# A cheaper score step in the attention's budget, a copy moved to ScalarE, and one more step between x row loads and their use

## The chip, the cores and the metric

The kernel runs on 1 core of one Trainium2 chip. The core has five engines with instruction queues of their own: TensorE (PE, with its weight loads shown apart as PEld), VectorE (DVE), ScalarE (ACT), GpSimd (POOL) and SyncE (SP), which here issues nearly all DMAs. The metric is the device time of one execution in microseconds; the time of a kernel is the median of its runs.

## The reference, cut to what matters

One layer of a streaming encoder for 1024 new frames ("prompt") and 64 further frames of a running stream ("sample"), 1088 tokens of width 1024 in all. Two half-step SwiGLU layers stand around the token mixers.

```python
x = x + 0.5 * g1 * swiglu(modulate(rms_norm(x, norm_f1), sh1, sc1), w_up1, w_down1)
hm = modulate(rms_norm(x, norm_mix), shm, scm)
q_a, k_a, v_a, q_r, k_r, v_r, z_r, gate_a, gate_r = jnp.split(hm @ w_in, offsets, axis=-1)
...
    o_a = diff_attention_prompt(q_a, k_a, v_a, lam)      # 4 heads, two softmaxes each
    o_r, s_new = retention_prompt(q_r, k_r, v_r, log_g)  # 4 heads
...
    o_a = diff_attention(q_a, k_all, v_all, pos, ...)    # sample: 2048 cached keys and values
    o_r, s_new = retention_block(q_r, k_r, v_r, past_s, log_g)
...
merged = jax.nn.sigmoid(gate_a) * (o_a @ w_a_proj) + jax.nn.sigmoid(gate_r) * (o_r @ w_r_proj)
x = x + gm * (merged @ w_o)
x = x + 0.5 * g2 * swiglu(modulate(rms_norm(x, norm_f2), sh2, sc2), w_up2, w_down2)
```

## The kernel before

Activations lie transposed, with features on the partitions. All big matrix products run in three passes, high times high, high times low and low times high (`mm3`, L162 to L164): every operand is split into two halves (`split`, L134 on ScalarE makes the high half, L138 the low one on GpSimd or VectorE). The tokens are worked in two groups, 0 to 511 and 512 to 1087 (`GRP`). The program is written in one order; the build then orders each engine's instructions by that order and by its own reckoning of what is ready, so instructions of neighbouring steps are mixed. An engine takes its instructions in the order so made. A tile with a given number of buffers is handed on when its last reader is done.

**First SwiGLU (`ffn`).** For each group, 22 iterations `up(j)` make seven products of 12 matmuls each for two columns of 128 features, and `down` multiplies pairs of iterations by the down weights, which are staged in the tile `raw` of `wraw` (two buffers). In `up`, `pump` calls the generator `side` behind each product: in group 0 seven times an iteration for j below 3 (`SIDE0`, `NS0`) and three times after (`SIDE`), 78 times in all. `down` of iterations 0 and 1 comes behind `up(2)`, that of 2 and 3 behind `up(4)`.

**Its side work (`side_work`).** The generator follows the pattern `PAT`, in which "g" is a step of the modulation vectors, "r" a step of `load_x` and "y" an end of the call; after the pattern, the rest of `load_x` runs at one step per call. `load_x(1, later)` brings in the second group's tokens as five rows of up to 128 tokens. Per row: a load into `xrow` (L727; one buffer, shared with the tile `g` that every third iteration of `up` writes), `WAIT` steps without work, eight transposes on TensorE (L742), copies into a `raw` tile of `wraw` (L745), a Square with its sum (L746), and a store to `xin` (L748). Behind it come `far_sums` for the second group and twelve steps for each of three modulation vectors.

**Into the mixers.** While the second group's `down` ends, `after1` squares x (ScalarE, L333) and adds the squares into `sqa[1]` (VectorE, L334). After it, one instruction copies `sqa[1]` into `sq1` (L862), so that the pools of the SwiGLU can be closed. `far_sums` turns `sq1` into the second group's norm: `rms_cols` multiplies it by ones on TensorE (L342).

**The mixers, group by group.** `w_in` is worked as pairs of 128 columns (`pair`): seven products, and a `tick` after each. The pairs that the mixers need come in the order of `ORDER`; where the number of live tiles doesn't allow the next, and at the end, pairs of the gates come (`fill`). The mixers themselves are tasks, generators that yield a delay in ticks and a cost:

```python
def tick(g):
    now[0] += 1
    credit[0] = min(credit[0] + RATE[g], RATE[g])
    for task in sorted(tasks, key=lambda task: task[0]):
        if credit[0] <= 0:
            break
        while task[0] <= now[0]:
            got = next(task[1], "end")
            ...
            credit[0] -= cost
```

`RATE` is 2.0 in both groups. Tasks are `att_core` (per head four score steps `scores`, with two reductions L1105 and two exponentials L1107 each, transposes L1137 and values L1123), in the second group `att_decode` (keys of the cache L1183 to L1189, weights L1204, values of the cache L1212), and the retention `ret_core` (L1260 to L1305, one step at a time in the tile S, which the scores use too and which has one buffer in the second group) with its outputs `ret_out` (L1315). When all pairs are done, `while tasks: tick(g)` runs what is left. Then the merge (`project`) begins, its first matmuls into the tile `acc`.

Of the kernel before, what the change touches and what calls it, by code (L numbers as in the profile page):

```python
# [34 lines left out]
DA, DB, DH, DR, DT, DX = 4, 1, 4, 2, 2, 2  # L35
UA = 12
DC, DK, DV, EARLY = 2, 2, 1, True
# [3 lines left out]
NB = len(BLK)  # L41
GRP = [(0, 512), (512, 576)]
BGRP = [[0, 1], [3, 2]]
NY, NV, NTT, SIDE0, SIDE, TAIL, SLACK, NRA, NS0, WAIT, NNEAR = 4, 2, 6, 7, 3, 2, 5, 3, 3, 1, 2
LOP = (1, 4)
NDG = 4
PAT = "gyry" * 8 + "g"
# [36 lines left out]
def encoder_layer(tc: tile.TileContext, a, o, stage=9):  # L84
    nc = tc.nc
# [10 lines left out]
    def close(*names):  # L96
        for name in names:
            guards.pop(name).__exit__(None, None, None)
# [27 lines left out]
    def misc():  # L126
        return psum["pool"].tile([P, 512], F32, tag="misc", name="misc", bufs=psum["misc"])
# [706 lines left out]
    sqa = {}  # L834
# [24 lines left out]
    phase(1)  # L859
    upool = pool("u")  # L860
    sq1 = upool.tile([P, 576], F32, tag="ft", name="sq1", bufs=NFT)
    nc.vector.tensor_copy(sq1, sqa[1])  # L862
    close("n1", "x1", "ps_f1", "acc")
    mpool = pool("mix", "right")
    spsum = pool("ps_mix", space=PSUM)
# [19 lines left out]
    def c4():  # L885
        return dec["pool"].tile([P, dec["c4"]], F32, tag="c4", name="c4", bufs=NC4)

    def small(n=P):
        return mpool.tile([P, n], F32, tag=f"s{n}", name="s", bufs=6 if n == P else 4 if n > P else 2)

    def col(n=1):
        return mpool.tile([P, 8], F32, tag="col", name="col", bufs=24)[:, :n]
# [4 lines left out]
    def st():  # L897

        return dec["ps"].tile([P, dec["st"]], F32, tag="S", name="S", bufs=2048 // dec["st"])
# [65 lines left out]
    def spawn(gen, delay=1):  # L965
        tasks.append([now[0] + delay, gen])
# [103 lines left out]
    def heads_out(rows, ss, n, w, dcols, dst):  # L1070

        f = rsqrt(ss[:w, :n], 1.0 / VD)
        for j in range(n):
            nc.scalar.mul(rows[:, j], rows[:, j], f[:w, j:j + 1])
        yield DH, 0.1
        ot = c4()
        t = misc()
        for j in range(4):
            nc.tensor.transpose(t[:, j * w:(j + 1) * w], rows[:, j], ident[:w, :w])
        for j in range(0, 4, 1 if len(dcols) > 1 else 4):  # L1080
            e = (j + 1 if len(dcols) > 1 else 4) * w
            nc.scalar.mul(ot[:, j * w:e], t[:, j * w:e], dcols[j % len(dcols)])
        for q, (d, a0, a1) in enumerate(dst):
            nc.sync.dma_start(d, ot[:, a0:a1])
        yield 1, 0.9

    def att_core(g, h, q, ks, v, done):

        rows, ss = [], col(8)

        def scores(r):
            w = P * (4 * g + r + 1)
            p, sums = [], col(2)
            t = st()
            half = dec["st"] // 2
            both = t[:, :half], t[:, half:]
            for k, k0 in ks:
                k1 = min(k0 + 512, w)
                for c, s in enumerate(both):
                    cs = slice(c * HD, (c + 1) * HD)  # L1100
                    nc.tensor.matmul(s[:, k0:k1], q[cs, r * P:(r + 1) * P], k[cs, :k1 - k0], start=True, stop=True)
            for c, s in enumerate(both):
                nc.vector.memset(s[:HD, w - HD:w], -1e30)
                nm, sm = col(), sums[:, c:c + 1]
                nc.vector.tensor_reduce(out=nm, in_=s[:, :w], op=ALU.max, axis=AX.X, negate=True)  # L1105
                e = c4()
                nc.scalar.activation(e[:, :w], s[:, :w], AF.Exp, bias=nm, accum_out=sm)  # L1107
                p.append(e)
            rs, cf = col(2), col()
            nc.vector.reciprocal(rs, sums)  # L1110
            r0, r1 = rs[:, 0:1], rs[:, 1:2]
            nc.vector.scalar_tensor_tensor(out=cf, in0=sums[:, 0:1], scalar=r1, in1=neglam, op0=ALU.mult, op1=ALU.mult)
            nc.vector.scalar_tensor_tensor(out=p[0][:, :w], in0=p[1][:, :w], scalar=cf, in1=p[0][:, :w],
                                           op0=ALU.mult, op1=ALU.add)
            return p, r0

        def values(r, at, r0):
            if not rows:
                rows.append(mpool.tile([P, 4, P], F32, tag="rows", name="rows", bufs=1))
            n = 4 * g + r + 1  # L1120
            t = misc()
            for j in range(n):
                nc.tensor.matmul(t[:, :P], at[:, j * P:(j + 1) * P], v[j], start=(j == 0), stop=(j == n - 1))  # L1123
            nc.scalar.mul(rows[0][:, r], t[:, :P], r0)
            nc.scalar.activation(small(), t[:, :P], AF.Square, scale=r0, accum_out=ss[:, r:r + 1])
            return 0.22 * n

        p, r0 = scores(0)
        yield DA, 0.0034 * 128 * (4 * g + 1)
        for r in range(4):  # L1130
            i = 4 * g + r
            at = p[1]
            for j0 in range(0, i + 1, 4):
                t = misc()
                n = min(4, i + 1 - j0)
                for j in range(n):
                    nc.tensor.transpose(t[:, j * P:(j + 1) * P], p[0][:, (j0 + j) * P:(j0 + j + 1) * P], ident)  # L1137
                nc.scalar.copy(at[:, j0 * P:(j0 + n) * P], t[:, :n * P])
            yield DB, 0.22 * (i + 1)
            cur = r, at, r0  # L1140
            if r < 3 and EARLY:
                p, r0 = scores(r + 1)
                if r == 2:
                    done()
                yield DC, 0.0034 * 128 * (i + 2)
            cost = values(*cur)
            if r < 3 and not EARLY:
                p, r0 = scores(r + 1)
                if r == 2:
                    done()  # L1150
                cost += 0.0034 * 128 * (i + 2)
            yield DA - (DC if EARLY else 0), cost
        spawn(heads_out(rows[0], ss, 4, P, [dcol[:, h:h + 1]], [(osp_a[h][:, g * 512:g * 512 + 512], 0, 512)]))

# [183 lines left out]
    for g in range(2):  # L1338
# [9 lines left out]
        def attend():  # L1348
            for h in range(HEADS):
                yield from until(("q", h), ("v", h))  # L1350
                ks, vs = [(got["k", h], 512 * g)], [got["v", h][:, j] for j in range(4)]
                if g:
                    ks.insert(0, (kv(ksp[h]), 0))
                    va = kv(vsp[h]).rearrange("p (j c) -> p j c", c=P)
                    vs = [va[:, j] for j in range(4)] + vs
                    yield 3, 0.1
                yield from att_core(g, h, got["q", h], ks, vs, lambda: free("q", h))
                free("v", h)
# [25 lines left out]
        while lins or rest:  # L1384
            if lins and live[0] + lins[0][0] <= dec["u"]:
                n, f, i = lins.popleft()
# [120 lines left out]
    sqa = npool.tile([P, 576], F32, tag="yf", name="sqa", bufs=NY)  # L1507
# [97 lines left out]
```

## Time and profile before

| | |
|---|---|
| median of 3 runs | 2578.6 us (2573.17 to 2580.3) |
| the profiled execution | 2576.09 us, span 2574.3 us |
| mean granted TensorE clock | 0.981 |
| busy: PE, DVE, POOL, ACT | 2446.7, 1818.7, 1618.6, 1125.2 us |

The span runs from the first to the last instruction of the profiled execution. Busy time of an engine is the time in which at least one of its instructions runs; idle time before an instruction is put down to what released it. The granted clock is a share of the full one.

### The profile page before, as it was taken

Reading aid. Unit: us, or ns where it says so; the run is one execution under the profiler, and the core shown is the slowest. Engines: PE = TensorE matmul, PEld = TensorE weight load, DVE = VectorE, ACT = ScalarE, POOL = GpSimd, SP = SyncE. Lnnn points to the kernel's source line nnn. Section 1 sums busy time; section 2 is a strip of 40 time slices with the busy share of each in tenths; the row PEclk is TensorE's granted clock in tenths of the full one; section 3 lists DMA queues with packets and bytes.
Section 4 is the critical chain, followed back from the end, with each engine's and each line's share of the span. In section 5 each row is a group of like instructions: output and inputs, shape, how many; then the busy total and the mean of one; then the engine's idle time right before and its main releaser. Section 6 shows DMA issues by size and latency. Waiting matters only on the chain. (4 is left out here: it accounts for less than half of the span.)

```text
span 2574.3 us, 45302 instructions
## 1 busy us (share of the span) xinstructions
PE 2446.7 (95%) x17278; PEld 2259.9 (88%) x17278; DVE 1818.7 (71%) x3132; ACT 1125.2 (44%) x1928; POOL 1618.6 (63%) x1058
## 2 busy tenths in 40 slices
PE   6999999999999889998999998999999999999998
PEld 3888889999999778887878986798889998999998
DVE  5586667776666897787665664557877777766766
ACT  4443335443334445553445545534444444333333
POOL 5796676887666466686444533655767665756562
PEclk9999999999999999999999998999999999999999
DMA  8655445554443553543333336646453335323331
GB/s 284 218 189 157 141 153 194 176 152 146 140 137 102 179 172 117 170 154 113 109 110 104 117 98 203 197 130 220 122 166 106 99 101 185 112 91 91 91 91 38
DMA packets 425005, 365.25 MB, mean 142 GB/s; under 512 B 18780, under 2 KB 358420, under 8 KB 424788
## 3 DMA queue, kind: packets, MB, share of 16 engines
q1 hardware_dynamic: 424608, 362.28, 45.3%
q8 instruction: 137, 2.24, 0.4%
q14 instruction: 80, 0.66, 0.1%
q10 hardware_dynamic: 180, 0.06, 0.0%
HBM read 307.95 MB, written 52.10 MB: 140 GB/s over the span
## 5 line engine op out<-in xcount | busy, mean ns | idle before, releaser
L162 PE MATMUL misc<-h,whi 128*128 128x288 f32 (+2 forms) x3360 | 1010.8, 301 | 32.8 <-DVE t L518 15.8
L164 PE MATMUL misc<-h,wlo 128*128 128x288 f32 (+2 forms) x3360 | 988.7, 295 | 9.7 <-DVE wlo L138 6.7
L163 PE MATMUL misc<-h,whi 128*128 128x288 f32 (+2 forms) x3360 | 990.0, 295 | 5.1 <-DVE h L138 5.0
L162 PEld LDWEIGHTS misc<-h,whi 128*128 128x128 f32 x3360 | 645.7, 192 | 72.4 <-DVE t L518 18.5
L164 PEld LDWEIGHTS misc<-h,wlo 128*128 128x128 f32 x3360 | 645.6, 192 | 16.4 <-DVE wlo L138 8.1
L163 PEld LDWEIGHTS misc<-h,whi 128*128 128x128 f32 x3360 | 645.8, 192 | 14.9 <-DVE h L138 7.1
L138 POOL TENSOR_TENSOR wlo<-raw,whi 128x1024 fp32r<-128x1024 f32 x150 | 374.7, 2498 | 270.3 <-ACT whi L134 236.2
L518 DVE TENSOR_TENSOR t<-misc,t 128x256 f32<-128x256 f32 (+1 forms) x560 | 235.0, 432 | 235.0 <-PE misc L164 202.0
L138 DVE TENSOR_TENSOR wlo<-ws,whi 128x1024 fp32r<-128x1024 f32 x178 | 313.5, 1761 | 62.4 <-ACT whi L134 61.1
L138 POOL TENSOR_TENSOR wd<-raw,wd 128x512 fp32r<-128x512 f32 x176 | 233.6, 1349 | 100.5 <-ACT wd L134 100.4
L653 DVE SCALAR_TENSOR_TENSOR x<-misc,gate,x 128x288 f32<-128x288 f32 (+3 forms) x540 | 239.8, 486 | 52.5 <-PE misc L164 45.1
L134 ACT CAST whi<-ws 128x1024 fp32r<-128x1024 f32 x178 | 186.7, 1049 | 203.6 <-PE misc L163 125.7
L134 ACT CAST whi<-raw 128x1024 fp32r<-128x1024 f32 x160 | 167.4, 1046 | 215.3 <-PE misc L163 170.8
L518 POOL TENSOR_TENSOR ws<-raw 128x512 f32<-128x512 f32 x134 | 192.4, 1438 | 98.9 <-DVE wlo L138 60.6
L134 ACT CAST wd<-raw 128x512 fp32r<-128x512 f32 x176 | 102.7, 619 | 186.9 <-PE misc L164 172.0
L162 PE MATMUL misc<-h,wd 128*128 128x288 f32 (+3 forms) x552 | 178.8, 327 | 5.1 <-DVE t L518 3.1
L163 PE MATMUL misc<-h,wd 128*128 128x288 f32 (+3 forms) x552 | 178.6, 325 | 0.0
L164 PE MATMUL misc<-h,wd 128*128 128x288 f32 (+3 forms) x552 | 176.4, 324 | 0.0
L518 POOL TENSOR_TENSOR h<-raw 128x512 f32<-128x512 f32 x78 | 109.7, 1407 | 84.1 <-issue 34.5
L162 PE MATMUL misc<-h,wb 128*128 128x256 f32 (+1 forms) x512 | 151.5, 296 | 5.2 <-ACT h L134 4.2
L163 PE MATMUL misc<-h,wb 128*128 128x256 f32 (+1 forms) x512 | 148.9, 291 | 0.0
L164 PE MATMUL misc<-h,wb 128*128 128x256 f32 (+1 forms) x512 | 148.9, 291 | 0.0
(297 smaller groups left out, 4787.2 us busy)
## 6 DMA issues: line engine op xcount, KB each, us to landing
raw<-in_w_up_dram SPq DMA_DIRECT2D x176, 512.0 KB, 4.0
raw<-in_w_down_dram SPq DMA_DIRECT2D x88, 512.0 KB, 4.0
raw<-in_w_in_dram SPq DMA_DIRECT2D x80, 512.0 KB, 4.0
rawa<-in_w_ada_dram SPq DMA_DIRECT2D x24, 1024.0 KB, 6.6
h<-in_w_ada_dram SPq DMA_DIRECT2D x16, 512.0 KB, 7.0
raw<-in_w_o_dram SPq DMA_DIRECT2D x16, 512.0 KB, 4.3
raw<-far SPq DMA_DIRECT2D x14, 576.0 KB, 3.7
yf<-xsp SPq DMA_DIRECT2D x24, 288.0 KB, 4.3
```

Source lines behind the costliest of these rows:

```text
L134: nc.scalar.copy(hi, src)
L138: eng.tensor_tensor(out=lo, in0=src, in1=hi.bitcast(F32), op=ALU.subtract)
L162: nc.tensor.matmul(out, wh, xh, start=first, stop=False)
L163: nc.tensor.matmul(out, wh, xl, start=False, stop=False)
L164: nc.tensor.matmul(out, wl, xh, start=False, stop=last)
L518: eng.tensor_tensor(out=out, in0=in0, in1=in1, op=op)
L653: nc.vector.scalar_tensor_tensor(out=xm, in0=t[:, c0 - cs.start:c1 - cs.start], scalar=gate()[:, m, s:s + 1], in1=xm, op0=ALU.mult, op1=AL ...
```

## The change

Three edits. In `att_core`, the cost that a score step yields to the budget is 0.0018 per column where it was 0.0034, in all its places; no other cost changes. The copy of `sqa[1]` into `sq1` is issued to ScalarE and not to VectorE. `WAIT` is 2 and not 1, so in `load_x` two steps without work lie between a row's load and its transposes; the first group's rows don't pass through it.

```diff
-NY, NV, NTT, SIDE0, SIDE, TAIL, SLACK, NRA, NS0, WAIT, NNEAR = 4, 2, 6, 7, 3, 2, 5, 3, 3, 1, 2
+NY, NV, NTT, SIDE0, SIDE, TAIL, SLACK, NRA, NS0, WAIT, NNEAR = 4, 2, 6, 7, 3, 2, 5, 3, 3, 2, 2
...
     sq1 = upool.tile([P, 576], F32, tag="ft", name="sq1", bufs=NFT)
-    nc.vector.tensor_copy(sq1, sqa[1])
+    nc.scalar.copy(sq1, sqa[1])
...
         p, r0 = scores(0)
-        yield DA, 0.0034 * 128 * (4 * g + 1)
+        yield DA, 0.0018 * 128 * (4 * g + 1)
...
-                yield DC, 0.0034 * 128 * (i + 2)
+                yield DC, 0.0018 * 128 * (i + 2)
             cost = values(*cur)
             if r < 3 and not EARLY:
                 p, r0 = scores(r + 1)
                 if r == 2:
                     done()
-                cost += 0.0034 * 128 * (i + 2)
+                cost += 0.0018 * 128 * (i + 2)
```

`EARLY` is true, so the last of these lines isn't reached.

## Rows read from the trace of the kernel before

**Rows 1.** The page: busy time, share of the span, instructions of each engine.
```profile
PE 2446.7 (95%) x17278; PEld 2259.9 (88%) x17278; DVE 1818.7 (71%) x3132; ACT 1125.2 (44%) x1928; POOL 1618.6 (63%) x1058
```
**Rows 2.** Windows: stretch and its length, busy time by engine, clock, DMA.
```profile
872.00:880.00 8.00, 7.68 (x36) 7.65 (x37) 7.97 (x16) 2.78 (x7) 6.24 (x5) 0.50 0.71 205
50.00:100.00 50.00, 42.54 (x275) 34.59 (x275) 28.39 (x44) 24.18 (x42) 36.08 (x21) 0.90 0.70 217
850.00:900.00 50.00, 41.82 (x305) 40.36 (x304) 44.07 (x85) 22.73 (x44) 26.18 (x17) 0.90 0.63 195
1550.00:1600.00 50.00, 40.25 (x235) 32.27 (x234) 23.36 (x55) 27.91 (x56) 19.78 (x18) 0.86 0.69 228
1220.00:1556.00 336.00, 324.66 (x2291) 284.01 (x2291) 216.27 (x387) 160.64 (x314) 157.97 (x104) 0.99 0.35 106
```
**Rows 3.** TensorE's waits over the whole span: us in total, times, longest.
```profile
PE misc L1212 <- DMA ck<-in_cache_v_dram: 2.4, 2, 2.1
...
PE S L1101 <- ACT c L1107: 1.4, 3, 0.7
...
PE S L1279 <- ACT c L1107: 1.0, 1, 1.0
```
**Rows 4.** Timeline of TensorE after the last fill pair: start, us, instructions.
```profile
1558.74 3.68 PE L1204 MATMUL misc<-s,P 128*128 128x64 f32 x32
...
1566.22 1.91 PE L1212 MATMUL misc<-ck,c 128*64 128x128 f32 x16
1570.20 1.09 PE L1212 MATMUL misc<-ck,c 128*64 128x128 f32 x8 [2.06 <-DMA ck<-in_cache_v_dram]
...
1581.85 0.79 PE L1315 MATMUL misc<-ident,s 64*128 64x64 f32 x2 [6.24 <-DVE s L1305]
...
1584.93 0.79 PE L162 MATMUL acc<-h,whi 128*128 128x512 f32 x1
```
**Rows 5.** Timeline of all engines around the copy L862.
```profile
870.41 0.41 DVE L334 TENSOR_TENSOR sqa<-sqa,sq 128x256 f32<-128x256 f32 x1
...
870.57 1.04 ACT L134 CAST whi<-h 128x1024 fp32r<-128x1024 f32 x1 [2.42 <-DVE h L518]
...
871.08 1.19 DVE L862 COPY sq<-sqa 128x576 f32<-128x576 f32 x1
...
872.32 1.01 PE L342 MATMUL misc<-ones,sq 128*128 128x1 f32 x4 [4.50 <-DVE sq L862]
```
**Rows 6.** Groups by form: one of min/median/max ns, two with busy us and mean ns.
```profile
L134 ACT CAST h<-u x14: 667/672/678, 1147.2 to 1158.2; 128x576 fp32r<-128x576 f32 x14
...
L1105 DVE TENSOR_REDUCE col<-S 128x1 f32<-128x1024 f32 x8 | 9.7, 1218 | 0.1
...
L1107 ACT ACTIVATE c<-S,col 128x1024 f32<-128x1024 f32 x8 | 8.9, 1113 | 4.5 <-DVE col L1105 4.5
```
**Rows 7.** Timeline of SyncE's DMA issues from 84 to 99.
```profile
86.12 0.53 SPq L748 DMA_DIRECT2D xin<-raw  x1
87.08 1.83 SPq L727 DMA_DIRECT2D xrow<-in_x_sample_dram  x1
...
93.97 0.54 SPq L748 DMA_DIRECT2D xin<-raw  x1
97.95 0.35 SPq L629 DMA_DIRECT2D raw<-in_w_down_dram  x1
```
**Rows 8.** Timeline of TensorE around the fourth and fifth x rows.
```profile
82.83 0.28 PE L162 MATMUL misc<-h,whi 128*128 128x256 f32 x1
...
84.27 1.04 PE L742 MATMUL misc<-ident,xrow 128*128 128x128 f32 x8
...
92.36 1.08 PE L742 MATMUL misc<-ident,xrow 64*128 64x64 f32 x8 [3.62 <-DMA xrow<-in_x_sample_dram]
93.37 0.58 PE L162 MATMUL misc<-h,whi 128*128 128x256 f32 x1
...
98.66 0.30 PE L162 MATMUL misc<-h,wb 128*128 128x256 f32 x1
```

## The prediction

> **What bounds the kernel now.** I read the page first: TensorE is busy for 2446.7 us of the 2574.3 us span [rows 1]. That leaves 127.6 us, so a change off TensorE can only win idle time, or time in which TensorE ran at the lower of its two clock levels. Then the windows, at the places that the edits touch [rows 2]: TensorE idles about 7.5 us from 50 to 100, 8.2 from 850 to 900 and 9.8 from 1550 to 1600, with a mean granted clock of 0.86 to 0.90. From 1220 to 1556, nearly the whole second mixer group, it idles only 11.3 us in 336. Last, what ended each wait: the last x row (3.62 us before L742), the copy of the sums of squares (4.50 us before L342), cached values (2.06 us before one L1212 group) and the end of the retention (6.24 us before L1315) [rows 8, 5, 4].
>
> **Edit 1, the score price.** I followed the tick rule through both groups with both prices, step by step. In group 0 (140 ticks) the budget never postpones a task, so every step stays on its tick. In group 1 (ticks 141 to 291, last pair begun at 274) it does. Of its four heads, 0 and 1 move: pair q1 is begun one pair earlier, so head 1's first score step falls on tick 186, not 193. Heads 2 and 3 stay. The decode steps of the last head come about 6 ticks earlier: its two large weight steps at 275 and 277, not 281 and 282; its four value steps at 279 to 282, not 285 to 288. The last retention steps stay (276 to 286).
>
> After tick 280 no fill matmuls are left, and this tail is what changes. In the trace it runs from about 1558.7 to the first merge matmul at 1584.93 [rows 4]. The two weight steps (3.68 us for 32 matmuls) and half of the value matmuls (1.91 us for 16) go in front of the last products: 5.6 us of TensorE, which cost the same there, so this gains nothing by itself. What goes is the wait for cached values, 2.06 us before the group at 1570.20 and 0.3 before the next, 2.4 in all: with products in between, the loads have time. No earlier head has such a wait, since the waits list has two in the whole run, and they are these [rows 3]. The 6.24 us at L1315 stay: the retention steps that feed it keep their ticks. Value: -2.4 us. Bounds: the L1315 gap goes too, -8.6 us; or the shuffled ticks of heads 0 and 1 cost as much again as their stretch now idles, +11.3 us.
>
> **Edit 2, the copy.** On VectorE it takes 1.19 us, from 871.08, and TensorE starts L342 at 872.32 [rows 5]. Its input's last add begins at 870.41 and takes 0.41 us. ScalarE takes 0.672 us for 128x576 elements, the median of 14 casts [rows 6], and is in a cast of 1.04 us from 870.57 [rows 5]. If the copy is placed ahead of that cast, it runs from about 870.9 to 871.6: -0.7 us. If behind, it ends at 872.3: nothing. The cast behind it would lose up to 1 us. It makes the weights of a later pair, and TensorE is busy for 7.68 us of 872 to 880 [rows 2], so that is covered; without this cover it costs that 1 us. VectorE's queue moves up by 1.19 us, covered in the same way. Value: -0.4 us, bounds -0.7 and +1.0.
>
> [...]
>
> **Edit 3, the x rows.** `xrow` has one buffer, so a load can only go out when the row before has been squared: the fourth row's transposes begin at 84.27, the fifth's load goes out at 87.08, and its transposes begin at 92.36 [rows 7, 8]. The edit does not move the loads ahead; it puts the transposes later, after side calls 6, 12, 17, 20 and 23, not 4, 8, 12, 16 and 18 (one call behind each of the seven products of the first three iterations, then three per iteration). From one row's transposes to the earliest next is 92.36 - 84.27 = 8.1 us. Today two products lie between the last two rows, and TensorE waits 3.62 us. Then it runs two products of 12 matmuls from 93.37 to 98.66, 5.29 us, where one took 1.44 us before (82.83 to 84.27): 2.4 us lost to the lower clock [rows 8]. After the edit the tightest place is between the third and the fourth row, with three products, so the wait is 3.62 - 1.44 = 2.2 us. After the 2.06 us wait in the tail, eight matmuls took 1.09 us where sixteen had taken 1.91 [rows 4], so I take no clock loss. The last row comes behind the whole down step and waits for nothing. Gain: 3.6 - 2.2 + 2.4 = 3.8 us.
>
> Against this stands what queues behind. A transposed row is staged in one of two `raw` buffers, which the down weights take next. The fourth row's store goes out at 86.12, 1.85 us after its transposes begin; today's second down tile is loaded at 97.95, 3.98 us after the fifth row's store [rows 7]. After the edit the third row stands one product behind today's fourth, at 84.27 + 1.44 = 85.7, and the fourth at 93.8. Its store goes out at 95.7 and the second down tile is loaded at 99.7, 1.7 us later than today, while TensorE would reach the down step almost 4 us earlier. The first tile alone feeds 8 banks with 3 matmuls of 512 columns, an estimated 0.24 us each (0.12 for 256, from the 1.44 us): 5.8 us. So of the 3.8 us gained some 2 to 3 are waited away; I take 2.6. The side chain behind the rows comes 5 calls later, 72 of 78, so it still ends in place. The third iteration's `g` tile waits for the last row too; its down step is two iterations on. Value: -3.8 + 2.6 = -1.2 us. Bounds: no wait is left at all, -6.0; or the down weights bring a wait of 3.6 us and 2.4 of lower clock, +2.2.
>
> **Sum.** -2.4 - 0.4 - 1.2 = -4.0 us. The profiled execution took 2576.1 us (span 2574.3); the median of the runs is 2578.6, 2.5 above. So 2572.1 against the profiled one and 2574.6 against the median, which I predict.
>
> **The rivals.**
>
> *The waits go entirely* (faster). The build orders TensorE's instructions by its own reckoning, and may put the fourth row behind the third iteration's last product, and the last retention steps among the products that the decode steps pushed back. For it: both gaps are single waits with ready work behind them. Against: today's fifth row stood in program order, and was waited for. Price: -6.0 for the rows, -8.6 for the tail, -0.7 for the copy: -15.3, 2563.3 us.
>
> *The score bank becomes the bound* (slower). In group 1 the tile S has one buffer, shared by score and retention steps. A score step holds it through two reductions and two exponentials, the largest 1.22 and 1.11 us each [rows 6]; an estimate with the two engines overlapping is 3.4 us. By the tick rule, a score and a retention step stand within one tick of each other 4 times today and 7 times after, twice in the same tick. Three more such waits, each with 2.4 us of lower clock, are 17 us: 2574.6 + 17 = 2591.6. Against: TensorE's waits for S behind an exponential are 1.4 us in 3 places and 1.0 in one [rows 3], so it mostly has other matmuls. It decides if two of the three new places leave TensorE without any for over 3 us.
>
> *The edits do next to nothing.* Each gap comes back under another name: the row wait as one for down weights, the wait for values as one for the retention. Sum 0, 2578.6 us. For it: the retention chain that ends the tail isn't moved.
>
> **How the numbers follow.** A difference under 0.3%, 7.7 us, is about what a measurement here can tell from none: the runs of before span 2573.17 to 2580.3. Chances: forecast 0.36, nothing 0.18, waits gone 0.30, score bank or down weights 0.16. Faster by more than 0.3% (below 2570.9) is the third and a little of the forecast's edge, 0.31. Slower (above 2586.3) is most of the last, 0.15. Same: 0.54. The range leaves out the far part of the score bank's case and a little below the best: 2562 to 2587. The forecast's own is 2569 to 2580.
>
> **What would show it.** Right: L742's largest wait near 2 us or gone, and the clock up from 93 to 99; L862 on ScalarE near 0.67 us and L342's wait at most 4.5; no wait before L1212 in the tail, fewer matmuls in it, and L1315's gap still there. Wrong: a new wait of a down matmul for `wd` near 100 us; waits of L1101, L1260 or L1279 behind L1107 or L1305 beyond 3 us; much more than 11.3 us idle between 1220 and 1556.

## The result, and the profile after

The changed kernel takes 2607.07 us (median of 4 runs, 2600.16 to 2612.38) where the kernel before took 2579.45 in the same comparison: 1.0101 times as long, 95% interval 1.0081 to 1.0121. That is 1% slower, and above the predicted range. Three single executions well above the others of their kernel (3349.79 us of the kernel before, 10038.33 of price_head0 and 2633.35, the traced one, of price_dear) are left out of every ratio and mean below. The profiled execution has a span of 2605.2 us, 30.9 more than that of before. The page's line of busy times, which answers to [rows 1]:

```profile
PE 2464.9 (95%) x17278; PEld 2273.2 (87%) x17278; DVE 1821.2 (70%) x3131; ACT 1127.3 (43%) x1929; POOL 1620.6 (62%) x1058
```

TensorE does the same 17278 matmuls and is busy 18.2 us longer, at a lower mean clock (0.973, before 0.981; every record of the granted clock in the two traces is 1.00 or 0.50); the other 12.7 us are idle time. To see where, I cut TensorE's stream of both kernels at the places where it has done equal amounts of its work (each matmul counted with the median duration of its shape), so that a stretch of one kernel stands against the same work in the other. Windows of the kernel before; after each stretch and its length come busy us (and instructions) of PE, PEld, DVE, ACT and POOL, then clock and DMA:

```profile
0.00:191.20 191.20, 165.09 (x1039) 131.66 (x1040) 125.57 (x203) 90.25 (x154) 136.35 (x96) 0.96 0.72 231
191.20:843.50 652.30, 643.54 (x4690) 605.13 (x4688) 451.05 (x775) 263.43 (x403) 466.73 (x304) 1.00 0.48 150
843.50:1181.20 337.70, 307.29 (x2296) 284.92 (x2296) 287.12 (x534) 166.07 (x343) 222.86 (x136) 0.95 0.51 158
1181.20:1280.10 98.90, 91.69 (x631) 80.72 (x630) 70.80 (x107) 44.78 (x84) 52.14 (x34) 0.98 0.35 103
1280.10:1406.70 126.60, 122.42 (x870) 105.92 (x868) 76.00 (x146) 58.86 (x118) 58.89 (x41) 1.00 0.36 107
1406.70:1549.60 142.90, 140.39 (x991) 122.67 (x991) 93.61 (x166) 69.66 (x138) 65.28 (x42) 1.00 0.35 106
1549.60:1633.10 83.50, 73.75 (x384) 60.09 (x383) 39.90 (x74) 43.33 (x78) 34.08 (x26) 0.92 0.65 207
1633.10:2574.30 941.20, 902.58 (x6388) 868.85 (x6387) 674.64 (x1131) 388.82 (x615) 582.30 (x382) 0.98 0.39 121
```

The same work in the changed kernel:

```profile
0.00:204.30 204.30, 172.01 (x1047) 137.72 (x1048) 132.88 (x201) 90.89 (x154) 132.06 (x95) 0.94 0.65 210
204.30:856.80 652.50, 643.20 (x4682) 603.33 (x4680) 446.09 (x777) 264.95 (x402) 473.19 (x305) 1.00 0.49 152
856.80:1197.00 340.20, 309.50 (x2296) 286.99 (x2296) 284.81 (x533) 166.43 (x344) 221.34 (x136) 0.94 0.51 157
1197.00:1290.60 93.60, 90.02 (x633) 79.66 (x632) 65.42 (x107) 44.57 (x84) 48.50 (x32) 0.98 0.35 101
1290.60:1426.90 136.30, 126.82 (x864) 109.66 (x864) 79.49 (x150) 60.19 (x122) 61.58 (x43) 0.95 0.34 103
1426.90:1573.60 146.70, 142.30 (x999) 124.57 (x997) 95.81 (x164) 69.53 (x136) 67.47 (x44) 0.99 0.35 105
1573.60:1659.90 86.30, 75.53 (x384) 60.37 (x384) 38.88 (x71) 41.06 (x73) 35.61 (x24) 0.90 0.63 197
1659.90:2605.20 945.30, 905.55 (x6389) 870.95 (x6387) 677.81 (x1133) 389.72 (x616) 580.79 (x382) 0.98 0.39 121
```

The lengths differ by +13.1, +0.2, +2.5, -5.3, +9.7, +3.8, +2.8 and +4.1 us. The first stretch holds the x rows and the side chain (edit 3), the third edit 2, and the fourth to the seventh are the second mixer group and its tail (edit 1). The third and the last also vary between kernels in which TensorE has the same order there, as a table below shows, so their 2.5 and 4.1 us are no evidence.

**The x rows.** Timeline of TensorE in the changed kernel, two extracts, to be read against [rows 8]:

```profile
97.40 1.65 PE L742 MATMUL misc<-ident,xrow 128*128 128x128 f32 x8 [3.30 <-DVE wlo L138]
102.57 0.50 PE L162 MATMUL acc<-h,wd 128*128 128x512 f32 x1 [1.11 <-ACT wd L134]
109.62 0.50 PE L162 MATMUL acc<-h,wd 128*128 128x512 f32 x1 [1.32 <-ACT wd L134]
...
175.14 0.50 PE L162 MATMUL misc<-h,wd 128*128 128x512 f32 x1 [1.25 <-DVE t L518]
180.70 0.79 PE L162 MATMUL misc<-h,wd 128*128 128x512 f32 x1 [3.89 <-DVE v L518]
```

Timeline of SyncE's issues there, for [rows 7]:

```profile
91.16 2.07 SPq L727 DMA_DIRECT2D xrow<-in_x_prompt_dram  x1
95.96 0.34 SPq L629 DMA_DIRECT2D raw<-in_w_down_dram  x1
...
103.69 0.33 SPq L629 DMA_DIRECT2D raw<-in_w_down_dram  x1
```

The wait for a row has moved from the fifth to the fourth and is 3.30 us, hardly less than 3.62. The row's load is issued at 91.16, lands 6.1 us later, and its transposes start 6.2 us later; the VectorE instruction named as releaser ends at about the same time. The lower clock behind the wait is there too: the granted clock is 0.61 from 98 to 102, where it is 0.50 from 92 to 98 in the kernel before. Behind it two waits for down weights are new (the second tile is loaded at 103.69, 5.7 us later than before), and then two near 180 us, behind VectorE.

**The copy.** All lines are from timelines of the changed kernel, for [rows 5]:

```profile
884.83 0.41 DVE L334 TENSOR_TENSOR sqa<-sqa,sq 128x256 f32<-128x256 f32 x1
...
885.33 0.67 ACT L862 COPY sq<-sqa 128x576 f32<-128x576 f32 x1 [2.66 <-DVE sqa L334]
...
886.05 1.76 PE L342 MATMUL misc<-ones,sq 128*128 128x1 f32 x8 [4.11 <-ACT sq L862]
```

From the end of the last add to L342 it is now 0.81 us (885.24 to 886.05), before 1.50 (870.82 to 872.32).

**Head 1 and the tail.** TensorE's timeline in the second mixer group; the lines from 1589.45 on answer to [rows 4]:

```profile
1352.55 0.44 PE L1279 MATMUL S<-u,s 64*64 64x128 f32 x4 [2.06 <-ACT c L1107]
...
1355.97 1.75 PE L1137 MATMUL misc<-ident,c 128*128 128x128 f32 x7 [1.18 <-DVE c L1113]
...
1375.59 1.94 PE L1137 MATMUL misc<-ident,c 128*128 128x128 f32 x8 [3.36 <-DVE c L1113]
...
1589.45 0.49 PE L1260 MATMUL S<-u 64*128 64x128 f32 x4
...
1593.71 1.09 PE L1212 MATMUL misc<-ck,c 128*64 128x128 f32 x8 [0.17 <-DMA ck<-in_cache_v_dram]
...
1598.20 0.33 PE L1260 MATMUL S<-u 64*64 64x64 f32 x4
...
1606.16 0.47 PE L1315 MATMUL misc<-ident,s 128*128 128x128 f32 x1 [3.70 <-ACT s L1316]
...
1610.79 1.24 PE L1079 MATMUL misc<-ident,drows 64*128 64x64 f32 x4 [1.87 <-ACT drows L1074]
1612.38 0.79 PE L162 MATMUL acc<-h,whi 128*128 128x512 f32 x1 [0.35 <-ACT s L1316]
```

A retention step waits for the tile S behind head 1's exponentials, and head 1's transposes (L1137) wait twice for its softmax: 6.6 us, and the clock of this stretch is 0.95 where it was 1.00. In the kernel before the wait for S was 1.0 us [rows 3], and these transposes waited 1.5 us (TensorE's waits from 1200 to 1480):

```profile
PE misc L1137 <- DVE c L1113: 1.5, 2, 0.9
```

In the tail the wait for cached values is gone (0.17 us), as forecast, but the last retention step (L1260) now begins behind the last values, and the merge begins 14.2 us behind it. In the kernel before it began ahead of the last values, 13.4 us before the merge:

```profile
1562.47 0.49 PE L1260 MATMUL S<-u 64*128 64x128 f32 x4
...
1571.58 0.33 PE L1260 MATMUL S<-u 64*64 64x64 f32 x4
...
1572.51 1.09 PE L1212 MATMUL misc<-ck,c 128*64 128x128 f32 x8 [0.36 <-DMA ck<-in_cache_v_dram]
```

From the last but one retention step to the merge it is 22.5 us in the kernel before (1562.47 to 1584.93) and 22.9 in the changed one (1589.45 to 1612.38). The waits for values lay inside this time, and it is no shorter without them.

### The profile page after: what moved, and what is told of

It reads as the page before. It is cut to its first block, busy times and chain, and to the rows that moved or that the text cites. A ratio compares the mean times of both kernels' runs of the same rounds, so it can differ in the third digit from the quotient of the medians.

```text
span 2605.2 us, 45289 instructions
## 1 busy us (share of the span) xinstructions
PE 2464.9 (95%) x17278; PEld 2273.2 (87%) x17278; DVE 1821.2 (70%) x3131; ACT 1127.3 (43%) x1929; POOL 1620.6 (62%) x1058
## 5 line engine op out<-in xcount | busy, mean ns | idle before, releaser
L518 DVE TENSOR_TENSOR t<-misc,t 128x256 f32<-128x256 f32 (+1 forms) x560 | 235.1, 432 | 237.8 <-PE misc L164 208.9
L138 DVE TENSOR_TENSOR wlo<-ws,whi 128x1024 fp32r<-128x1024 f32 x178 | 319.3, 1794 | 59.8 <-ACT whi L134 59.6
L653 DVE SCALAR_TENSOR_TENSOR x<-misc,gate,x 128x288 f32<-128x288 f32 (+3 forms) x540 | 240.9, 487 | 66.7 <-PE misc L164 59.3
L518 POOL TENSOR_TENSOR ws<-raw 128x512 f32<-128x512 f32 x134 | 194.0, 1450 | 101.5 <-DVE wlo L138 64.2
L518 POOL TENSOR_TENSOR h<-raw 128x512 f32<-128x512 f32 x78 | 109.4, 1404 | 82.4 <-issue 24.4
```

The lines of the kernel that those rows point to most:

```text
L138: eng.tensor_tensor(out=lo, in0=src, in1=hi.bitcast(F32), op=ALU.subtract)
L518: eng.tensor_tensor(out=out, in0=in0, in1=in1, op=op)
L653: nc.vector.scalar_tensor_tensor(out=xm, in0=t[:, c0 - cs.start:c1 - cs.start], scalar=gate()[:, m, s:s + 1], in1=xm, op0=ALU.mult, op1=AL ...
```

## The experiments

Each was timed against the kernel before on the same chip, in five rounds. Every execution also reports its span and mean granted clock, so the difference of the mean spans can be split: span times (1 - clock) is my estimate of what the clock took at most (TensorE's idle time at the lower clock counts in it too), the rest is work and waiting. Mean differences to before, with a standard error of 1 to 2 us, of up to 3 in the changed kernel with its four executions (it is set against all runs of before, mean span 2578.4):

```
kernel             ratio   95% interval      span  clock  rest
changed kernel     1.0101  1.0081 to 1.0121 +26.3  +15    +11
wait_alone         1.0049  1.0032 to 1.0065 +13.3   +3.4   +9.8
price_alone        1.0049  1.0031 to 1.0067 +14.3   +6.4   +7.8
copy_alone         1.0004  0.9992 to 1.0016  +0.8   -0.6   +1.5
wait_chain_back    1.0034  1.0017 to 1.0050  +9.4   -0.2   +9.5
chain_late         1.0011  0.9998 to 1.0023  +2.7   -0.5   +3.1
chain_early        1.0017  1.0004 to 1.0030  +4.8   +0.9   +3.8
last_row_alone     1.0001  0.9989 to 1.0013  +0.3   -4.1   +4.4
wait_dense         1.0028  1.0015 to 1.0041  +7.8   +0.6   +7.2
price_head0        1.0054  1.0037 to 1.0070 +12.9  +11.5   +1.4
price_rest         1.0027  1.0017 to 1.0037  +6.2   +2.3   +3.9
price_q1_late      1.0032  1.0018 to 1.0046  +8.3   +4.7   +3.6
price_h1_room      1.0024  1.0009 to 1.0040  +6.3   +6.1   +0.1
price_dear         1.0053  1.0031 to 1.0075 +14.4  +12.5   +1.9
q1_late_tail_held  1.0033  1.0019 to 1.0046  +7.9   +5.9   +2.0
h1_room_tail_held  1.0039  1.0024 to 1.0055 +10.4  +10.5   -0.1
all_with_repairs   1.0049  1.0034 to 1.0065 +13.1   +4.1   +9.0
```

And the eight stretches of equal work in the profiled execution of some of them, us (worked out as above; the last ends with the last matmul):

```
before            191.2 652.3 337.7  98.9 126.6 142.9  83.5  933.8
changed kernel    204.3 652.5 340.2  93.6 136.3 146.7  86.3  937.8
wait_alone        204.1 652.7 342.6  98.6 126.1 142.9  82.7  938.5
wait_chain_back   199.9 651.4 340.6  99.1 126.3 142.9  81.8  930.0
chain_late        196.5 652.4 340.4  97.7 127.4 142.9  84.2  938.0
copy_alone        191.4 653.8 347.7  98.6 126.0 142.9  83.1  935.5
price_alone       190.6 654.0 344.9  94.2 135.7 146.7  84.7  937.8
price_head0       192.9 650.7 348.1  94.3 140.9 142.4  83.2  936.5
price_rest        189.3 652.0 341.1  99.0 126.7 145.8  87.7  934.0
price_q1_late     189.9 651.5 340.5  94.0 131.5 145.5  88.6  930.5
price_h1_room     192.9 651.1 346.7  94.2 131.0 145.0  83.5  932.9
q1_late_tail_held 191.1 653.4 340.0  94.5 132.8 147.2  85.1  934.3
wait_dense        202.1 651.8 340.7  98.4 126.6 142.9  82.2  933.3
```

The third and the last column show how much one execution differs from the next without any cause in the kernel: price_head0 has TensorE's order of before up to 1206 us, and the copy of before, and yet its profiled execution is 10.4 us longer in the third stretch (348.1 for 337.7). In the first column of the table kernels with TensorE's order of before lie between 189.3 and 192.9, in the fourth to the seventh they agree within 1 to 3 us. So a single stretch is read for 4 us or more in the first column and for 3 or more in the fourth to the seventh.

**Each edit alone.** Theory A: each edit loses at the place that it moves. Theory B: the prediction's own terms. Theory C: any new order loses somewhere by chance.

```diff
-NY, NV, NTT, SIDE0, SIDE, TAIL, SLACK, NRA, NS0, WAIT, NNEAR = 4, 2, 6, 7, 3, 2, 5, 3, 3, 1, 2
+NY, NV, NTT, SIDE0, SIDE, TAIL, SLACK, NRA, NS0, WAIT, NNEAR = 4, 2, 6, 7, 3, 2, 5, 3, 3, 2, 2
```

> Only the x rows' two steps. Theory A (each loss sits at the place that its edit moves): TensorE's stream of the changed kernel is 4 us late behind the first down step and 13 us late near 200 us, and 11 to 13 at the end of the first group; this kernel shows the same, so 2588 to 2592 us, about +11. Theory B (the working of the prediction: what waits for the rows and the down weights is all of it): -1 us, 2578. Theory C (any reshuffle of the instructions' order moves the time by chance, all over the kernel): the loss is not found before 430 us.

1.0049, and its profiled execution loses 12.9 us in the first stretch, as much as the mean difference. TensorE's order differs from that of before between 47 and 399 us only; the second stretch, with the later part of this, loses nothing.

```diff
-        yield DA, 0.0034 * 128 * (4 * g + 1)
+        yield DA, 0.0018 * 128 * (4 * g + 1)
...
-                yield DC, 0.0034 * 128 * (i + 2)
+                yield DC, 0.0018 * 128 * (i + 2)
```

> Only the score step's price. Theory A: the first 1180 us are those of before; then -4 to -5 us near 1240, +10 from 1350 to 1380, +3 to +8 behind it, so +9 to +16 us, 2588 to 2595. Theory B: -2.4 us, 2577. Theory C: the loss is spread over stages that the edit doesn't reach, and the three single edits do not add up to the 28 us of the whole change.

1.0049: -4.7 us in the fourth stretch, +9.1 in the fifth, +3.8 and +1.2 behind it, the changed kernel's own pattern.

```diff
-    nc.vector.tensor_copy(sq1, sqa[1])
+    nc.scalar.copy(sq1, sqa[1])
```

> Only the copy on ScalarE; TensorE's order is that of before. Prediction's step: -0.4 us (bounds -0.7 and +1.0), the wait of L342 4.1 us where it was 4.5. [...]

1.0004, nothing that can be told from zero. The three sum to 1.02%, the whole change measures 1.01%: the edits add up, each at its own place. Their clock parts don't (9 us in sum, 15 in the whole change), so the split between clock and rest is known to some us only. B falls, and C as far as it says that the loss lies all over the kernel.

**Rows and side chain apart.** With two steps, rows and side chain both come later. The steps without work that `far_sums` has before its banks move the chain alone (10 of them in `chain_late`, none in `chain_early`, both with one step between the rows; none in `wait_chain_back`, with two):

```diff
-        for _ in range(SLACK):
+        for _ in range(SLACK if own is not False else 10):
```

> One step between x rows as in the kernel before, but ten steps without work ahead of the side chain's normalisation, not five, so that the chain comes five calls later as it does behind the late rows. Theory A with the side chain as the cause: the rows' wait of 3.62 us stays, a stall of 4 to 5 us with lower clock behind it comes near 175 us, +7 to +9 us, 2586 to 2588. Rival (late rows are the cause): within 1.5 us of the kernel before.

> Two steps between x rows, but the five steps without work ahead of the side chain's normalisation are left out, so that this chain comes at the same calls as in the kernel before; the rows stay late. Theory A with the side chain as the cause of the stall near 180 us: what is lost is the 4 us up to the end of the first down step, so +2 to +5 us, 2581 to 2584, and no wait over 2 us near 180. Rival (the late rows themselves shift the down weights and everything behind): as late as the kernel with the two steps alone, +11 us.

> The kernel before, but with none of the five steps without work ahead of the side chain's normalisation, so that the chain comes five calls earlier and the rows stay. If the chain's lateness costs evenly (3 us for five calls later), this gains up to 3 us; if what costs is only where it meets the down step, or its own input from the last row, it is within 2 us of before or slower by as much.

Late chain 2.7 us, late rows 9.4, both 13.3: nearly the sum. I had it the other way round, with the chain as the main cause. The stall that I had tied to the chain is there with the chain alone (timeline of TensorE in chain_late):

```profile
172.69 0.79 PE L162 MATMUL misc<-h,wd 128*128 128x512 f32 x1 [3.10 <-DVE t L518]
```

but it is the smaller part. An earlier chain loses too (4.8 us), so there is no even price per call. Its longest new wait is also behind VectorE (2.87 us behind an L518, before a product at 131.42); that the chain costs by what it meets there is what these two traces suggest, and no run isolates it.

```diff
-                for _ in range(WAIT):
+                for _ in range(WAIT + (q == n - 1)):
```

> Two steps without work only ahead of the last row (64 tokens), one ahead of the others; the side chain comes one call later. If the prediction's idea of the edit is right in itself, the wait of 3.62 us shrinks to about 2 us or less and nothing else moves: -2 to -5 us, 2575 to 2578. Theory A' (each late row puts the down weights, the store and the VectorE work behind it later, and TensorE meets them again): no gain, 0 to +5 us.

The row's wait shrank to 2.36 us and the clock gave back 4.1 us, but 4.4 us of other waits came in their place (1.11 and 1.38 us for down weights, 2.44 us behind VectorE at 161): 1.0001.

```diff
-                up(j, SIDE0 if j < NS0 and not g else SIDE)
+                up(j, SIDE0 + 2 * (first is not None) if j < NS0 and not g else SIDE)
```

> Two steps between x rows, but 9 side calls in each of the first three iterations of the first group, not 7, so that the rows' transposes stand 4.7, 9.3, 13.2, 15.6 and 17.9 products into it (4, 8, 12, 16 and 18 before) and the side chain is one call ahead of its place. Theory A (the second step costs only by the lateness of rows and chain): within 0 to +4 us of before. Rival (the second step costs by what it does between the rows, as one more wait): +9 us or more.

1.0028, +7.8 us, between theory and rival and nearer the rival: some 5 of 13 us come back with the lateness. The rows' wait is then longer than in any other kernel (timeline of TensorE in wait_dense):

```profile
93.74 1.94 PE L742 MATMUL misc<-ident,xrow 128*128 128x128 f32 x8 [5.78 <-DMA xrow<-in_x_prompt_dram]
101.58 0.69 PE L742 MATMUL misc<-ident,xrow 64*128 64x64 f32 x8 [1.54 <-ACT misc L595]
```

**Which step of the price.** By the tick rule head 0's price alone begins pair q1 earlier.

```diff
-        yield DA, 0.0034 * 128 * (4 * g + 1)
+        yield DA, (0.0034 if h else 0.0018) * 128 * (4 * g + 1)
...
-                yield DC, 0.0034 * 128 * (i + 2)
+                yield DC, (0.0034 if h else 0.0018) * 128 * (i + 2)
```

> The lower price only for the score steps of head 0; by the tick rule this alone begins pair q1 one pair earlier and puts head 1's score steps 7 ticks earlier, while the tail is that of before. Theory A (the loss of the price hangs on head 1's steps falling among the decode and retention steps, where TensorE waits for the softmax of the one tile S): most of the 14 us of the price alone, so +9 to +14 us, 2589 to 2594, with waits of L1137 behind L1113 and of L1279 behind L1107 of 7 to 8 us together near 1350 to 1375. Rival (the loss comes from the tail or is spread): under +4 us.

1.0054, as expected, with 14.3 us lost in the fifth stretch and 4.6 gained in the fourth; the waits are nearly the forecast ones, 6.9 us together, but from 1332 on. TensorE's three longest there:

```profile
1332.24 0.44 PE L1279 MATMUL S<-u,s 128*64 128x128 f32 x4 [1.95 <-ACT c L1107]
1336.02 1.51 PE L1137 MATMUL misc<-ident,c 128*128 128x128 f32 x6 [1.68 <-DVE c L1113]
...
1356.13 0.69 PE L1279 MATMUL S<-u,s 64*64 64x128 f32 x4 [2.92 <-ACT c L1107]
```

The counterpart has the two prices the other way round (`0.0018 if h else 0.0034`):

> The lower price only for heads 1 to 3; by the tick rule the score steps of head 0 stay and pair q1 begins where it did. Theory A: no stall at head 1, and in the tail the two waits for cached values go as the prediction had it, so between -4 and +2 us, 2576 to 2582. Rival (the price costs wherever steps are let in earlier): +5 us or more.

1.0027: head 1's stretch is that of before (126.7 us), but 2.9 us are lost in the next and 4.2 in the tail. That the tail would gain was wrong, and +6.2 us is what the rival gave. The two parts, 12.9 and 6.2 us, sum to more than the 14.3 of the price alone, so they don't simply add.

```diff
-            if lins and live[0] + lins[0][0] <= dec["u"]:
+            late = g and lins and lins[0][1] is att_lin and lins[0][2] == 1 and len(rest) > len(fills) - 2
+            if lins and live[0] + lins[0][0] <= dec["u"] and not late:
```

> The lower price for all heads, but pair q1 is held back until the second pair of the gates is begun, as in the kernel before; by the tick rule head 1's steps then stand on the ticks of before (193 to 212), and only the last steps of head 0 and the tail move. Theory A (two separate losses: head 1's early steps some 9 us, the tail some 4 to 6 us, as the lower price for heads 1 to 3 alone measured): +4 to +7 us, 2585 to 2588, with no wait of L1279 or L1137 over 1.5 us between 1330 and 1380. Rival (the lower price costs 14 us however q1 stands): +11 us or more.

1.0032, at the upper edge of what the theory gave; a wait of 2.80 us for S behind an exponential is left near 1321, so holding q1 back doesn't restore the old order.

```diff
+        wait = DA + (g == 1 and h == 1)
-        yield DA, 0.0034 * 128 * (4 * g + 1)
+        yield wait, 0.0018 * 128 * (4 * g + 1)
...
-            yield DA - (DC if EARLY else 0), cost
+            yield wait - (DC if EARLY else 0), cost
```

> The lower price, pair q1 early as in the changed kernel, but in the second group head 1's transposes come 5 ticks behind their score step, not 4 (191 to 209, not 190 to 205). Theory A1 (what is lost at head 1 is the wait of the transposes for a softmax that VectorE and ScalarE have not finished in 4 ticks): the waits of L1137 behind L1113 at head 1 shrink below 1 us and 4 to 8 us come back, +6 to +10 us over before. Rival A2 (what is lost is the tile S, handed between score and retention steps): the waits of L1279 behind L1107 stay at 2 us or more and the time is that of the price alone, +12 to +15 us.

1.0024; 4.7 us come back in the fifth stretch. All of TensorE's waits of more than 0.6 us between 1310 and 1400 (lines from 1090 on are one higher in this kernel):

```profile
1333.80 0.33 PE L1261 MATMUL S<-u 64*64 64x64 f32 x4 [1.96 <-ACT c L1108]
1335.40 1.52 PE L1138 MATMUL misc<-ident,c 128*128 128x128 f32 x6 [0.96 <-DVE c L1114]
1359.59 0.98 PE L1138 MATMUL misc<-ident,c 128*128 128x128 f32 x7 [1.11 <-DVE c L1114]
```

One tick more takes most of the transposes' wait away, 2.1 us for 5.7 in price_alone (A1), and leaves most of the one for S, 2.0 for 2.8 (A2): both are there. Its interval overlaps that of price_alone at the edge.

```diff
-        yield DA, 0.0034 * 128 * (4 * g + 1)
+        yield DA, 0.0050 * 128 * (4 * g + 1)
...
-                yield DC, 0.0034 * 128 * (i + 2)
+                yield DC, 0.0050 * 128 * (i + 2)
```

> A dearer score step, 0.0050 per column. By the tick rule pair q1 and head 1's score steps stay within a tick of before, and the last steps come up to 3 ticks later. Theory A (only the two places cost: head 1's early steps and the order in the tail): within -2 and +5 us, the second from a longer tail. Rival (any other price reshuffles the second mixer group and loses): +6 us or more.

1.0053: a dearer step loses as much as a cheaper one, as the rival had it. So a loss of this size needs no step that comes earlier; theory A's two places were too narrow, and the weaker form of theory C, that any new order of this mixer group loses, is not excluded. The only trace of this kernel is of the execution left out above, so its times are not read. Its order is: behind the last pair's products stand three retention steps (L1260 at 1603.09, 1615.79 and 1633.59), where the kernel before has two (1562.47 and 1571.58). That is the longer tail that theory A allowed for; how much of the 14 us it takes is not shown.

**The tail put back.** In the two kernels with the lower price above, the last head's cached steps are held:

```diff
-        yield DA, 0.3
+        yield DA + 6 * (h == HEADS - 1), 0.3
```

> The lower price, pair q1 held back as in price_q1_late, and the last head's steps behind its softmax of the cache held 6 ticks longer, so that its weight steps stand on ticks 281 and 282 and its value steps on 284 to 287, behind the last retention steps' places of before. Theory A (the tail's loss comes from value steps ahead of the last retention steps): the last retention matmuls L1260 come some 7 us before the first merge matmul again as in the kernel before, the tail's 4 to 5 us come back, and 0 to +4 us over before remain. Rival (it is the price itself): +7 us or more.

> The lower price, pair q1 early, head 1's transposes 5 ticks behind their scores as in price_h1_room, and the last head's cached steps held 6 ticks longer. Theory A: what is left of price_h1_room's +6 us is mostly the tail, so -2 to +3 us over before. Rival: +5 us or more.

1.0033 and 1.0039, no gain over the same kernels without it: waits for cached values are back (2.31 and 2.18 us), and the last retention step still comes behind the values, 8.1 and 10.7 us ahead of the merge (in the kernel before it is 13.4, not the 7 that I had written). Both times are what the rivals gave, and the theory of the tail's order was not confirmed.

> All three edits, with the denser side calls, head 1's room and the held tail. If the three places are all of the change's loss: -2 to +6 us over before, 2578 to 2586. Rival (losses elsewhere that the counter-measures don't touch): +12 us or more.

1.0049, +13.1 us: half of the change's loss is left, which is the rival's case. The three places are not all of it. No kernel tried here beats the one before.

## Why the prediction was wrong

**Edit 3 is the first step that failed: -1.2 us predicted, +13 measured.** Three of its terms. First, the wait for a row was to shrink to 2.2 us because the third row would stand at 85.7 and the row-to-row time would stay 8.1 us. That time was taken from the 64-token row, the fourth has 128 tokens and took 97.40 - 88.70 = 8.7; and the third row itself came 3 us later than I placed it, behind a step of the modulation vectors (L235 and L240, 84.14 to 88.70). So the wait only changed its row, 3.30 for 3.62, and the 2.4 us of lower clock didn't come back in full either. Second, the down weights' waits came as listed and in the size that I took, 1.1 + 1.3 = 2.4 us for 2.6. Third, what lies behind was priced at nothing: "so it still ends in place". The runs with rows and chain apart put 9 us on late rows and 3 on the late chain. In the trace of the changed kernel TensorE's waits behind VectorE's L518 from 100 to 192 us are 6.8 us, 1.4 in the kernel before; in the whole first stretch 6.2 us of new idle time come with 6.9 of longer busy time.

One reason why VectorE is late there can be read, though no run isolates it. First line VectorE's timeline, the others GpSimd's, changed kernel:

```profile
126.80 5.67 DVE L138 TENSOR_TENSOR wlo<-ws,whi 128x1024 fp32r<-128x1024 f32 x1
...
126.33 1.30 POOL L138 TENSOR_TENSOR g<-v,g 128x512 fp32r<-128x512 f32 x1
127.59 1.29 POOL L518 TENSOR_TENSOR ws<-ws,raw 128x512 f32<-128x512 f32 x1
128.84 2.54 POOL L138 TENSOR_TENSOR wd<-raw,wd 128x512 fp32r<-128x512 f32 x2
```

Such a subtract takes 1.21 us when GpSimd is idle (at 163.45). This one ended at 132.47, 1.1 us after the last of four GpSimd instructions in a row (131.38). It is an extreme case of what the whole trace shows. Of the changed kernel's 227 subtracts of this shape into `wlo`, 139 began while a GpSimd instruction (one that had begun, or began within 0.05 us) had more than 0.2 us to run, and 136 of these ended 1.0 to 1.2 us after that instruction; the 88 others took 1.2 to 1.3 us. Groups by form, VectorE, 100 to 200 us, in the changed kernel (nine of them, mean 2558 ns) and in the kernel before (twelve, 1572 ns):

```profile
L138 DVE TENSOR_TENSOR wlo<-ws,whi 128x1024 fp32r<-128x1024 f32 x9 | 23.0, 2558 | 1.9 <-ACT whi L134 1.8
```

```profile
L138 DVE TENSOR_TENSOR wlo<-ws,whi 128x1024 fp32r<-128x1024 f32 x12 | 18.9, 1572 | 2.5 <-ACT whi L134 2.5
```

That one can end behind four such instructions in a row, and not only behind the first, the rows above show. What in the hardware makes it so, no run shows.

The longest wait, 3.89 us at 180.70, has no long subtract just ahead of it: from 171.18 on VectorE works without a pause at the chain's steps (L405, L413), the down step's L653 and the products' subtracts, and the L518 that TensorE waits for comes at 180.24.

**Edit 1 failed next: -2.4 us predicted, +14 measured.** The step was "Heads 2 and 3 stay", with heads 0 and 1 shuffled at no cost; the bound of +11.3 us that I set for the shuffle held the 8.2 us that the fourth to sixth stretches lost in the trace (-5.3 + 9.7 + 3.8), but I took zero. With the upper bounds of all three edits the sum would have been 2593 us, and my range ended at 2587; the result lies above both. The rival of the score bank named the place and nearly the size (17 us) and had too narrow a condition: no wait for S was over 3 us, but one of 2.06 and two of the transposes for the softmax in the same chain came together with lower clock; idle time between the same two times, 1220 and 1556, is 15.8 us for 11.3. The tail was the other half of this step. Its wait for values went, as forecast, but the path to the merge got no shorter. The last two retention steps and what follows them up to the merge take 22.9 us where they took 22.5 with the wait; in the eight other kernels with TensorE's order of before in the tail it is 22.1 to 23.3. In the place of the wait TensorE waits 0.87 and 1.59 us for the retention's outputs (before two L1315, at 1596.03 and 1597.94), which my rival of gaps that come back under another name had for this gap. So the value and weight steps that went in front cost their time there, and the stretch lost 2.8 us where 2.4 were to be gained. This is the reading of one trace: in the other lower-price kernels without a held tail that time is 20.7 to 25.2 us. Of the 14 us some 3 to 5 stay without a place: the traces show 9 (price_alone) to 11 us (changed kernel) in the four stretches, and my repair of the tail gave nothing back.

**The clock was left out of the price of waits in edit 1.** Of the changed kernel's 26 us, up to 15 are lower clock by the split above, with an error of about 3. I had read that the 2.06 us wait in the tail cost no clock and took small waits at their length. In the changed kernel's fifth stretch 5.3 us of new idle time come with 4.4 us of longer busy time at a granted clock of 0.95, in price_head0's 5.1 us with 9.4 at 0.93.

**Edit 2 was right as far as it can be read.** The copy takes 0.67 us on ScalarE and went ahead of the cast (at 885.91), the first of my two cases: from the end of the last add to L342 it is 0.81 us for 1.50, so -0.7, my bound, and not the -0.4 between the two cases. That L342's wait is 4.11 us for 4.50 looks like the forecast by luck, for in kernels that leave the copy on VectorE this wait is 3.7 to 5.2 us, and in copy_alone 3.76. The mean of copy_alone, +0.8 with 1.3 of error, can't tell the edit from zero. The copy's 1.19 us on VectorE may be another case of this. GpSimd's timeline in the kernel before:

```profile
870.56 1.39 POOL L518 TENSOR_TENSOR h<-raw,h 128x512 f32<-128x512 f32 x1 [0.63 <-DVE h L518]
```

It ran until 871.95, 0.87 us into the copy, which leaves 1.19 - 0.87 = 0.32 us for the copy by that reading, an estimate. The neighbours are the same in every trace with the copy on VectorE, so no run tests this.

## What to carry to other kernels

Where the bounding engine is busy 95% of the time, as here, moving steps of off-path work is not free (1.0101 times the time here): price each moved step by what it meets at its new place in every engine's queue, its DMAs and the GpSimd instructions beside a VectorE one (5.67 us for 1.21 here) included, and not by what it left behind. A wait is worth something only if it lies on the path that the next stage waits for (in the tail a wait of 2.06 us shrank to 0.17, and the path to the merge is 22.9 us for 22.5), and its price is not its length: in one stretch here 5.3 us of new idle time came with 4.4 us of longer busy time at a lower clock. And before a stretch of one trace is set against another's, look how far two executions with the same order differ in it: here up to 10 us.

## What the hardware showed that I had not expected

Executions with the same order of TensorE's instructions differ by up to 10 us in the stretch from 843 to 1181 us (337.7 in the kernel before, 348.1 in price_head0, which differs from it only behind 1200 us). And a VectorE subtract that takes 1.21 us alone took 5.67 us and ended 1.1 us after the last of four GpSimd instructions: the one that was running when it began and three more behind that one. In wait_alone the nine such subtracts from 100 to 200 us take 2450 ns in the mean, in the changed kernel's trace 2558.
